# Three passes of 256 columns against one of 512 and one of 256, on a float32r transformer kernel

## The chip, the core and the metric

The kernel runs on one core of a Trainium2 chip. TensorE multiplies (a weight load of 128 columns, then a pass in which the moving columns stream through), VectorE and ScalarE do elementwise work, GpSimd a few small powers, SyncE issues the loads of the weights. The metric is the device time of one execution in microseconds. The profile is that of one execution, with the span from its first to its last instruction.

## The reference

Two layers of a hybrid block and then two layers of a second block run over 256 tokens of width 1024, all in float32. What matters here is the matrix products; cut to them:

```python
h = modulate(rms_norm(x, norm1_g), shift1, scale1)          # first block, two layers
(rq, rk, rv, rg, gq, gk, gv, glr, gg, fq, fk, fv, ff) = split(h @ w_in)
...                                                          # retention, gated linear attention, fox attention
y_br = einsum('bsnw,nwd->bsnd', branches, w_br)
mixed = sum(sigmoid(h @ w_mg + b_mg) * y_br, axis=2) @ w_o
u, g = split(h2 @ w_up); u = causal_dwconv(u, w_conv, b_conv)
x = x + gate2 * ((silu(u) * g) @ w_down)                     # width 2816 in between
...
x = layer_norm(ALPHA * x + 0.5 * swiglu(x, wg, wu, wd))      # second block: twice per layer, a mixer between them
x = x + sigmoid(x @ ple_wg + b) * (p @ ple_wp)               # "ple" part
```

The modulation vectors (shift, scale, gate) are a matrix-vector product of the condition with `w_ada`.

## The kernel before

TensorE's fast format is float32r. To keep float32's accuracy, each operand is split into a high part in float32r and a low part, the rounded rest: weights as `wh` (ScalarE, L284) and `wl` (VectorE, L285), activations as a pair of tiles, `hh`/`hl` for the normed input, `bh`/`bl` for the input of a unit behind a norm, `hidh`/`hidl` for the hidden layer, `brh`/`brl`, `mxh`/`mxl`, `yh`/`yl`, `ph`/`pl` elsewhere. `mm3` (L329 to L331) then makes three passes, high x high, high x low and low x high, which add up in one PSUM region:

```python
mm(ps, wh, xh, start=first, stop=False, skip_group_check=True)
mm(ps, wh, xl, start=False, stop=False, skip_group_check=True)
i = mm(ps, wl, xh, start=False, stop=last, skip_group_check=True)
```

The work is cut into units of 256 output columns. A unit runs over 8 k-tiles of 128 rows (22 in the down projections), with two halves of 128 features each, so that a k-tile of a unit is two weight tiles of 128x128 and six passes. Kind F keeps features on partitions (the weights are loaded, 256 tokens stream); kind T keeps tokens on partitions (the activations are loaded, 256 weight columns stream), for the fox queries, keys and values and for the other values. A unit's sum stands in a tile `psg` of one PSUM bank, of which there are four, and a function (evac) takes it from there: a sigmoid, a convolution, a product, an update of the residual `x`. The other four banks are `psm` tiles, for the small products of the mixers. `pair_body` runs two units k-tile by k-tile. The first units behind a norm (`first_pair`) use `psw` tiles of 258 columns and are corrected by the norm's statistics afterwards (`norm_stats`, L490).

Weights come by DMA into six `raw` buffers of 512 KB, are split in chunks of 512 columns into ten pairs of `wh`/`wl`, and a chunk is asked for four chunks ahead. Extra work stands between the units: in the first block's gate stretch, and in its feed-forward, modulation products (`ada`, VectorE, L397), one 512 KB load each, whose results are needed later. In a gate block three gate units are followed by three branch units of 4 k-tiles each (`ybr`). Generators (`spawn`, `tick`) put the attention cores' small products in between the k-tiles. The instructions of an engine run in the order in which the tile framework puts them, and wait there for semaphores.

The order in a layer of the first block is: gated units behind the norm, the fox queries (a pair T), a small unit of 24 passes (`w_sm`), fox keys and values, the gated linear attention's units, the retention's units, four gate blocks, `w_o`, the feed-forward (22 up units, 4 down units).

## Time and profile before

| | |
|---|---|
| runs | 2084.49, 2087.77, 2089.73 us (median 2087.77) |
| profiled execution, span | 2080.2 us (no other time of it is recorded) |
| mean granted TensorE clock | 0.992 |
| TensorE busy | 2029.3 us, 16832 passes |
| VectorE busy | 1528.7 us |
| ScalarE busy | 1203.1 us |
| DMA | 402.87 MB, mean 194 GB/s |

Busy shares are unions of an engine's instructions. Successive matmuls overlap in the records (each lasts 280 ns or so), so that the pace of passes is to be read from the distance of their starts.

### The profile page before, as it was taken

The page shows a single profiled execution, that of the slowest core. Times are in us where ns is not written, and L with a number is a line of the kernel's source. Part 1 is how long each engine was busy: PE and PEld are TensorE (multiplying, and loading weights), DVE is VectorE, ACT ScalarE, POOL GpSimd, SP SyncE. Part 2 cuts the span into 40 slices and gives each one's busy share as a digit, 9 for nine tenths or more (in the row PEclk, how much of TensorE's full clock was granted, in tenths as well). Part 3 has the DMA queues.
Part 4 walks back from the last instruction along what each step waited for, and adds up shares of the span by engine and source line. Part 5 has one row for each costly group of instructions (what it writes and reads, how often), then busy time and mean ns, then how long its engine had stood idle before and what let it go on. Part 6 is the DMA issues. An engine that isn't in the chain of part 4 may idle for free.

```text
span 2080.2 us, 42872 instructions
## 1 busy us (share of the span) xinstructions
PE 2029.3 (98%) x16832; PEld 1996.0 (96%) x16832; DVE 1528.7 (73%) x2966; ACT 1203.1 (58%) x2268; POOL 42.3 (2%) x46
## 2 busy tenths in 40 slices
PE   6999999999999999999999999999999999999998
PEld 5999999999999999999999999999999998899998
DVE  7768789987668789865656798656765687587657
ACT  4755456555655456654555676555655586366545
POOL 0000000000000000000000000000000000000000
PEclk8999999999999999999999999999999999999999
DMA  8646876885546876765556436665566544246553
GB/s 314 203 142 230 279 255 220 291 277 182 166 143 231 280 251 220 226 180 191 187 179 187 156 117 203 185 185 169 193 187 182 178 153 123 82 147 193 182 171 105
DMA packets 123344, 402.87 MB, mean 194 GB/s; under 512 B 16994, under 2 KB 24452, under 8 KB 122884
## 3 DMA queue, kind: packets, MB, share of 16 engines
q1 hardware_dynamic: 112724, 396.71, 59.4%
q10 hardware_dynamic: 10416, 3.41, 0.7%
q8 instruction: 132, 2.16, 0.4%
q14 instruction: 72, 0.59, 0.1%
HBM read 396.79 MB, written 3.28 MB: 192 GB/s over the span
## 4 chain that ended last, share of the span: by engine, by line
PE 88%; DVE 6%; DMA 4%; issue 1%; POOL 1%; ACT 1%; SPq 0%; DVEq 0%; ACTq 0%; POOLq 0%
PE psg L329 26%; PE psg L330 26%; PE psg L331 26%; DMA raw<-w_ada 2%; PE psw L329 1%; PE psw L330 1%; PE psw L331 1%; DVE wl L285 1%; PE psm L1637 1%; DVE raw L397 1%; PE psm L1732 1%; PE psm L941 1%; DMA xx<-dx 1%; PE psm L1072 0%; DMA dx<-xb 0%
## 5 line engine op out<-in xcount | busy, mean ns | idle before, releaser
L284 ACT CAST wh<-raw 128x512 fp32r<-128x512 f32 (+1 forms) x1296 | 777.5, 616 | 641.3 <-PE psg L330 443.9
L285 DVE TENSOR_TENSOR wl<-raw,wh 128x512 fp32r<-128x512 f32 (+1 forms) x1296 | 867.0, 685 | 352.4 <-ACT wh L284 336.9
L330 PE MATMUL psg<-hl,wh 128*128 128x256 f32 x2328 | 652.8, 281 | 1.5 <-DVE hl L383 1.4
L329 PE MATMUL psg<-hh,wh 128*128 128x256 f32 x2328 | 653.0, 281 | 0.8 <-DVE gate L1180 0.8
L331 PE MATMUL psg<-hh,wl 128*128 128x256 f32 x2328 | 651.4, 280 | 1.3 <-DVE wl L285 1.3
L329 PEld LDWEIGHTS psg<-hh,wh 128*128 128x128 f32 x2328 | 437.8, 188 | 3.3 <-issue 2.0
L330 PEld LDWEIGHTS psg<-hl,wh 128*128 128x128 f32 x2328 | 438.2, 188 | 2.3 <-DVE hl L383 1.6
L331 PEld LDWEIGHTS psg<-hh,wl 128*128 128x128 f32 x2328 | 437.0, 188 | 1.7 <-DVE wl L285 1.5
L329 PE MATMUL psg<-hidh,wh 128*128 128x256 f32 x1056 | 297.2, 281 | 0.0
L330 PE MATMUL psg<-hidl,wh 128*128 128x256 f32 x1056 | 297.1, 281 | 0.0
L331 PE MATMUL psg<-hidh,wl 128*128 128x256 f32 x1056 | 297.1, 281 | 0.0
L329 PEld LDWEIGHTS psg<-hidh,wh 128*128 128x128 f32 x1056 | 198.8, 188 | 0.0
L331 PEld LDWEIGHTS psg<-hidh,wl 128*128 128x128 f32 x1056 | 198.8, 188 | 0.0
L330 PEld LDWEIGHTS psg<-hidl,wh 128*128 128x128 f32 x1056 | 198.8, 188 | 0.0
L330 PE MATMUL psg<-bl,wh 128*128 128x256 f32 x704 | 197.8, 281 | 0.2 <-DVE bl L383 0.2
L331 PE MATMUL psg<-bh,wl 128*128 128x256 f32 x704 | 197.6, 281 | 0.0
L329 PE MATMUL psg<-bh,wh 128*128 128x256 f32 x704 | 197.6, 281 | 0.0
L397 DVE CUSTOM_DVE_ANT_0 raw<-raw,cact,par 128x1024 f32<-128x1024 f32 x96 | 122.8, 1280 | 50.1 <-DMA raw<-w_ada 50.0
L330 PEld LDWEIGHTS psg<-bl,wh 128*128 128x128 f32 x704 | 132.8, 189 | 0.5 <-DVE bl L383 0.4
L329 PEld LDWEIGHTS psg<-bh,wh 128*128 128x128 f32 x704 | 132.8, 189 | 0.0
L331 PEld LDWEIGHTS psg<-bh,wl 128*128 128x128 f32 x704 | 132.6, 188 | 0.0
L329 PE MATMUL psg<-wh,hh 128*128 128x256 f32 (+1 forms) x368 | 106.5, 290 | 0.0
(436 smaller groups left out, 3007.5 us busy)
## 6 DMA issues: line engine op xcount, KB each, us to landing
raw<-f_up SPq DMA_DIRECT2D x176, 512.0 KB, 4.5
raw<-w_ada SPq DMA_DIRECT2D x96, 512.0 KB, 5.1
raw<-w_up SPq DMA_DIRECT2D x88, 512.0 KB, 5.2
raw<-w_in SPq DMA_DIRECT2D x80, 512.0 KB, 4.5
raw<-f_dn SPq DMA_DIRECT2D x80, 512.0 KB, 3.6
raw<-w_mg SPq DMA_DIRECT2D x48, 512.0 KB, 4.7
raw<-w_down SPq DMA_DIRECT2D x40, 512.0 KB, 3.8
raw<-c_in SPq DMA_DIRECT2D x32, 512.0 KB, 4.2
```

The costliest lines, as they stand in the source:

```text
L284: self.A.copy(out=wh[:, :e], in_=r)
L285: self.V.tensor_tensor(out=wl[:, :e], in0=r, in1=wh[:, :e].bitcast(F32), op=SUB)
L329: mm(ps, wh, xh, start=first, stop=False, skip_group_check=True)
L330: mm(ps, wh, xl, start=False, stop=False, skip_group_check=True)
L331: i = mm(ps, wl, xh, start=False, stop=last, skip_group_check=True)
L397: i = self.V.tensor_tensor_reduce(out=w, in0=w, in1=self.cact, scale=1.0, scalar=self.P(f"b_ada{l}", j), op0=MULT, op1=ADD, accum_out=self ...
L941: mm = lambda o, l_, r_, s, e: PE.matmul(o, l_, r_, start=s, stop=e, skip_group_check=True)
L1637: mm = lambda o, l_, r_, s: PE.matmul(o, l_, r_, start=s, stop=True, skip_group_check=True)
L1732: PE.matmul(p[:, i, :], l_(i, h), r_(i, h), start=(i == 0), stop=True, skip_group_check=True)
```

## The change

The two parts of an activation stand in one tile, `x[:, 0]` high and `x[:, 1]` low (`hx`, `bx`, `hidx`, `brx`, `mxx`, `yx`, `px`). A new kind A streams both through a weight tile in one pass of 512 columns, so that the first half of a PSUM bank gets high x high and the second half high x low, and adds low x high into the second half. Behind the unit `summed` copies the second half out of PSUM on ScalarE and adds the first on VectorE (tile `sm`), and the evac reads that. A `psg` tile is now two banks, and there are two of them. Kind T units are 512 columns wide and keep three passes; so do branch units, the small unit and the units behind a norm (kinds F and `mm3`). The weight pairs are eight in place of ten. The fox queries, keys, and the values are each one unit of 512 columns, with `both` and `whole` as their evacs. `down` and `wo` update `x` from `sm`; `ln_add` updates `x` twice from PSUM.

```diff
-    WB = 10
+    WB = 8
...
-        self.pg = pool("psg", bufs=4, space=PSUM)
+        self.pg = pool("psg", bufs=2, space=PSUM)
...
+    def mm2(self, ps, wh, wl, x, first, last):
+        self.mm(ps, wh, x, start=first, stop=False)
+        return self.mm(ps[:, 1, :], wl, x[:, 0, :], start=False, stop=last)
...
+    def kA(self, acc, wh, wl, x, first, last):
+        for m, ps in enumerate(acc):
+            sl = slice(m * 128, (m + 1) * 128)
+            self.mm2(ps, wh[:, sl], wl[:, sl], x, first, last)
...
+    def halves(self, t):
+        return [t[:, m, :].rearrange("p (z t) -> p z t", z=2) for m in range(2)]
+
+    def summed(self, u, out=None, scale=1.0):
+        acc, t = u
+        if out is None:
+            out = self.np_.tile([128, 2, S], F32, name="sm", tag="sm", bufs=3)
+        for hi, lo, o in self.parts(u, out):
+            if scale == 1.0:
+                self.A.copy(out=o, in_=lo)
+                self.V.tensor_tensor(out=o, in0=o, in1=hi, op=ADD)
...
-        return self.pg.tile([128, 2, S], F32, name="psg", tag="g")
+        return self.pg.tile([128, 2, 512], F32, name="psg", tag="g")
...
-        pa, pb = self.psG(), self.psG()
+        t = self.psG()
+        ua = (self.halves(t), t)
+        ub = ([self.psM((128, 2, S)) for _ in range(2)], None)
...
+    def ln_add(self, mp):
+        def fn(u):
+            x2 = self.x[:, 2 * mp:2 * mp + 2, :]
+            for hi, lo, x in self.parts(u, x2):
+                self.V.scalar_tensor_tensor(x, x, ALPHA, hi, MULT, ADD)
+                self.V.tensor_tensor(out=x, in0=x, in1=lo, op=ADD)
+            self.norm_add(mp)
...
-        self.pair(wi(0), wi(1), fox_qk("qF", 0, 0), fox_qk("qF", 1, 0), "T")
-        self.one(self.w(f"w_sm{l}", 0, 8, 128), small, m_n=1)
-        self.one(wi(2), fox_qk("kF", 0, 6), "T")
-        self.one(wi(3), fox_qk("kF", 1, 6), "T")
+        self.one(wt(0), both(fox_qk, "qF", 0), "T")
+        self.one(self.w(f"w_sm{l}", 0, 8, 128), small, "F", m_n=1)
+        self.one(wt(1), both(fox_qk, "kF", 6), "T")
```

How this moves instructions is shown at three places. The first is TensorE where a gate unit of the first layer ends and the first branch unit (`brh`, `brl`, then `brx`) begins; before:

```order
L331 MATMUL psg<-hh,wl 128x256
L329 MATMUL psg<-hh,wh 128x256
L330 MATMUL psg<-hl,wh 128x256
L331 MATMUL psg<-hh,wl 128x256
L329 MATMUL psg<-brh,wh 128x256
L330 MATMUL psg<-brl,wh 128x256
L331 MATMUL psg<-brh,wl 128x256
```

and of the change (L333 is `mm`, through which all passes go):

```order
L333 MATMUL psg<-hx,wh 128x512
L333 MATMUL psg<-hx,wl 128x256
L333 MATMUL psg<-hx,wh 128x512
L333 MATMUL psg<-hx,wl 128x256
L333 MATMUL psg<-brx,wh 128x256 x2
L333 MATMUL psg<-brx,wl 128x256
```

Two passes of the gate unit have become one of 512 columns; the branch unit still has three per weight tile. The second place is VectorE in the first layer's feed-forward, for a pair of units with two modulation products (`ISA raw,mod`); before:

```order
L285 TENSOR_TENSOR wl<-raw,wh 128x512 x2
L383 TENSOR_TENSOR hidl<-hid,hidh 128x512
L718 SCALAR_TENSOR_TENSOR conv<-psg,par,conv 128x255
L285 TENSOR_TENSOR wl<-raw,wh 128x512
L719 SCALAR_TENSOR_TENSOR conv<-psg,par,conv 128x254
L718 SCALAR_TENSOR_TENSOR conv<-psg,par,conv 128x255
L285 TENSOR_TENSOR wl<-raw,wh 128x512
L719 SCALAR_TENSOR_TENSOR conv<-psg,par,conv 128x254
L397 ISA raw,mod_82<-raw,cact,par 128x1024
L397 ISA mod_82 128x1
L285 TENSOR_TENSOR wl<-raw,wh 128x512
L728 TENSOR_TENSOR hid<-act,psg 128x512
```

and of the change:

```order
L404 TENSOR_TENSOR sm<-sm,psg 128x512
L290 TENSOR_TENSOR wl<-raw,wh 128x512
L450 ISA raw,mod_82<-raw,cact,par 128x1024
L450 ISA mod_82 128x1
L785 SCALAR_TENSOR_TENSOR conv<-sm,par,conv 128x255 x2
L786 SCALAR_TENSOR_TENSOR conv<-sm,par,conv 128x254 x2
L290 TENSOR_TENSOR wl<-raw,wh 128x512 x3
L404 TENSOR_TENSOR sm<-sm,psg 128x512
L290 TENSOR_TENSOR wl<-raw,wh 128x512
L795 TENSOR_TENSOR hid<-act,sm 128x512
```

An add (`sm`) has come ahead of each unit's evac, and everything else of it is still there. The third place is TensorE in the first layer around the small unit behind the fox queries; before, the query pair, the small unit and the keys follow each other with nothing between, and the turned queries (`w_486`, `w_496`, the two halves) stand later, within the keys:

```order
L330 MATMUL psg<-wl,hh 128x256
L331 MATMUL psg<-wh,hl 128x256
L903 MATMUL psm<-ident,w_486 128x128 x4
L903 MATMUL psm<-ident,w_496 128x128 x4
L329 MATMUL psg<-wh,hh 128x256
```

and of the change, from the end of the query unit over the small unit to the start of the key unit:

```order
L333 MATMUL psg<-wl,hx 128x512
L333 MATMUL psg<-wh,hx 128x512
L333 MATMUL psg<-hx,wh 128x256 x2
L333 MATMUL psg<-hx,wl 128x256
...
L333 MATMUL psg<-hx,wl 128x256
L975 MATMUL psm<-ident,w_434 128x128 x4
L333 MATMUL psg<-wh,hx 128x512
L333 MATMUL psg<-wl,hx 128x512
```

The turned first half of the queries (`w_434`) now stands ahead of the first pass of the keys.

## Rows read from the trace of the kernel before

**Rows 1.** The page, part 1: busy time and share of each engine.
```profile
PE 2029.3 (98%) x16832; PEld 1996.0 (96%) x16832; DVE 1528.7 (73%) x2966; ACT 1203.1 (58%) x2268; POOL 42.3 (2%) x46
```

**Rows 2.** Table of stretches: length, busy PE, PEld, DVE, ACT, POOL, clock, DMA share, GB/s.
```profile
139.20:181.30 42.10, 40.40 (x334) 39.58 (x332) 36.25 (x63) 22.24 (x38) 1.01 (x1) 1.00 0.59 190
206.90:232.40 25.50, 25.50 (x219) 25.50 (x218) 21.12 (x37) 11.98 (x25) 0.00 (x0) 1.00 0.86 290
306.40:322.60 16.20, 14.19 (x107) 13.98 (x106) 13.82 (x29) 9.47 (x20) 1.67 (x1) 0.89 0.63 212
322.60:435.70 113.10, 113.10 (x963) 113.10 (x962) 104.50 (x198) 66.66 (x129) 0.00 (x0) 1.00 0.81 271
...
791.10:904.20 113.10, 113.10 (x963) 113.10 (x962) 95.36 (x175) 73.45 (x133) 0.00 (x0) 1.00 0.69 216
...
966.80:1092.30 125.50, 125.50 (x1059) 125.50 (x1058) 75.02 (x122) 66.20 (x110) 0.00 (x0) 1.00 0.59 184
...
1683.50:1853.20 169.70, 157.28 (x1310) 152.31 (x1309) 124.66 (x334) 98.66 (x216) 11.62 (x9) 0.97 0.40 122
```

**Rows 3.** Timeline of TensorE: start, us, operation; steady stream, first and 23rd pass.
```profile
1675.79 0.28 PE L329 MATMUL psg<-hh,wh 128*128 128x256 f32 x1
...
1678.38 0.28 PE L330 MATMUL psg<-hl,wh 128*128 128x256 f32 x1
```

**Rows 4.** Timeline of TensorE: weights of 16 columns, first and 21st pass.
```profile
1679.96 0.28 PE L329 MATMUL psm<-hh,wh 128*16 128x256 f32 x1
...
1682.23 0.28 PE L331 MATMUL psm<-hh,wl 128*16 128x256 f32 x1
```

**Rows 5.** Timeline of TensorE: first passes of 128 columns behind longer ones.
```profile
1170.05 0.22 PE L329 MATMUL psg<-wh,hh 128*128 128x128 f32 x1
1170.11 0.28 PE L330 MATMUL psg<-wl,hh 128*128 128x128 f32 x1
```

**Rows 6.** Timeline of TensorE: token-major unit, first and ninth pass.
```profile
525.00 0.28 PE L330 MATMUL psg<-wl,hh 128*128 128x256 f32 x1
...
525.91 0.28 PE L329 MATMUL psg<-wh,hh 128*128 128x256 f32 x1
```

**Rows 7.** Timeline of TensorE: full float32 matmuls of 256 columns, ten and four in a row.
```profile
1203.88 2.32 PE L1306 MATMUL psm<-xb,bd 128*128 128x256 f32 x10
...
1206.74 1.02 PE L1306 MATMUL psm<-xb,bd 128*128 128x256 f32 x4
```

**Rows 8.** VectorE: timeline in the first feed-forward; all its waits for modulation weights.
```profile
360.50 1.28 DVE L397 CUSTOM_DVE_ANT_0 raw<-raw,cact,par 128x1024 f32<-128x1024 f32 x1
...
362.81 2.49 DVE L285 TENSOR_TENSOR wl<-raw,wh 128x512 fp32r<-128x512 f32 x4
...
DVE raw L397 <- DMA raw<-w_ada: 50.0, 22, 4.6
```

**Rows 9.** Timelines of TensorE, ScalarE, VectorE: small unit, fox queries leaving PSUM.
```profile
522.05 0.28 PE L329 MATMUL psg<-hh,wh 128*128 128x256 f32 x1
...
524.88 0.28 PE L329 MATMUL psg<-wh,hh 128*128 128x256 f32 x1
...
521.54 0.60 ACT L848 ACTIVATE w<-psg 128x512 f32<-128x512 f32 x1 [1.50 <-PE psg L331]
...
524.10 0.60 ACT L848 ACTIVATE w<-psg 128x512 f32<-128x512 f32 x1
...
528.55 0.69 DVE L896 TENSOR_TENSOR w<-psg,hr 128x512 f32<-128x512 f32 x1 [0.74 <-POOL hr L389]
```

**Rows 10.** Waits of TensorE: for what, us in total, times, longest.
```profile
PE psm L490 <- DVE sq L478: 9.0, 3, 4.8
```

**Rows 11.** Groups of instructions: residual update, busy us, mean ns, idle before.
```profile
L802 DVE SCALAR_TENSOR_TENSOR x<-x,psg 128x256 f32<-128x256 f32 x48 | 18.1, 418 | 4.8 <-PE psg L331 4.8
```

**Rows 12.** Timelines of ScalarE and VectorE: the end of the program.
```profile
2073.60 1.60 ACT L828 ACTIVATE sig<-psg,par 128x256 f32<-128x256 f32 x4 [1.54 <-PE psg L331]
...
2076.53 0.69 DVE L830 TENSOR_TENSOR x<-sig,x 128x512 f32<-128x512 f32 x1
```

More of the change, by code (lines that the diff above doesn't have):

```diff
@@ L185 @@
 class Prog:
-    DCH = 4
-    CH = 2
+    DMAX = 1024
     RAW = 6
-    WB = 10
+    WB = 8
     AHEAD = 4
@@ L243, in w, with ch @@
         ap, out = self.io[name][u], []
-        for k in range(0, kt, self.DCH):
-            kk = min(self.DCH, kt - k)
+        ch = self.ch(n)
+        dch = 2 * ch
+        for k in range(0, kt, dch):
+            kk = min(dch, kt - k)
             load = {"ap": ap[:, k * n:(k + kk) * n], "n": kk * n}
-            out += [("w", load, h * n, min(self.CH, kk - h), n) for h in range(0, kk, self.CH)]
+            out += [("w", load, h * n, min(ch, kk - h), n) for h in range(0, kk, ch)]
         return out
+    def ch(self, n=256):
+        return min(2, self.DMAX // 2 // n)
     def dump(self, name, t):
@@ L362, in unit, with parts @@
                 self.kT(*a)
+        return ps
+    def halves(self, t):
[8 more added lines that the diff above has]
+                self.V.tensor_tensor(out=o, in0=o, in1=hi, op=ADD)
+            else:
+                self.A.activation(o, lo, AF.Copy, scale=scale)
+                self.V.scalar_tensor_tensor(o, hi, scale, o, MULT, ADD)
+        return out
+    def parts(self, u, out):
+        acc, t = u
+        if t is None:
+            return [(a[:, 0, :], a[:, 1, :], out[:, m, :]) for m, a in enumerate(acc)]
+        return [(t[:, :, 0:S], t[:, :, S:2 * S], out)]
     def queue(self, on=True):
@@ L578, in corrected, with first_sums @@
         return c
+    def first_sums(self):
+        t = self.psG()
+        self.nk["st"], self.nk["sp"] = self.psM(), self.psM()
+        return [[t[:, m, 0:S + 2] for m in range(2)], [self.psM()[:, 0:S + 2] for _ in range(2)]]
     def first_pair(self, ca, cb, fa, fb, mid=None, at=(2, 3)):
@@ L627, in fn @@
             xg, g, b = nk["bh"], nk["g"], nk["b"]
-            pm = [[pool.tile([128, S + 2], F32, name="psw", tag=tag) for _ in range(2)] for pool, tag in ((self.pg, "g"), (self.pm, "m"))]
+            pm = st["pm"]
             for k in range(8):
@@ L757, in ffn_first @@
         for mp in range(4):
-            self.one(self.w(f"w_down{l}", mp, KF), down(mp), xs=lambda: (st["hh"], st["hl"]))
+            self.one(self.w(f"w_down{l}", mp, KF), down(mp), xs=lambda: st["h"])
         self.close(es)
@@ L820, in keep, with fn @@
         def keep(mp):
-            return lambda ps: self.A.copy(out=st["pp"][:, 2 * mp:2 * mp + 2, :], in_=ps)
+            def fn(u):
+                self.summed(u, st["pp"][:, 2 * mp:2 * mp + 2, :])
+            fn.raw = True
+            return fn
         def gate(mp):
@@ L906, in fox_qk, with whole @@
             return fn
-        def keepT(dst, u, n=512):
+        def whole(dst):
             def fn(ps):
-                if u == 0:
-                    b[dst] = T([128, 2, n], F32, "vT" if n == 512 else dst, 2 if n == 512 else 1)
-                A.copy(out=b[dst][:, :, u * 256:(u + 1) * 256], in_=ps)
+                b[dst] = T([128, 2, 512], F32, "vT", 2)
+                A.copy(out=b[dst], in_=ps)
             return fn
@@ L1127, in mix @@
         self.step([], cores)
-        self.one(wi(6), gq)
-        self.one(wi(7), gk, "T")
-        self.one(wi(8), keepT("gv", 0), "T")
-        self.one(wi(9), keepT("gv", 1), "T")
+        self.one(wi(0), gq)
+        self.one(wi(1), gk, "T")
+        self.one(wt(3), whole("gv"), "T")
         def core(*gens):
@@ L1333, in fn @@
                     b["ge"] = T([128, 4, S], F32, "ge")
-                A.copy(out=b["ge"][:, 2 * u:2 * u + 2, :], in_=ps)
+                self.summed(ps, b["ge"][:, 2 * u:2 * u + 2, :])
+            fn.raw = True
             return fn
@@ L1453, in out_proj @@
         w = [self.w(name, mp) for mp in range(4)]
-        f = [lambda ps, mp=mp: self.ln_add(ps, mp) for mp in range(4)]
+        f = [self.ln_add(mp) for mp in range(4)]
         self.pair(w[0], w[1], f[0], f[1], xs=xs, settle=4)
```

237 lines of the change are left out of this document (124 added, 113 removed).

## The prediction, made blind

> **What bounds the kernel now.** The first view is the page's table of engines: TensorE is busy for 2029.3 of 2080.2 us [rows 1]. The table of stretches shows that this holds nearly everywhere: in the twenty units of a feed-forward part, from 322.6 to 435.7, 960 weight passes and three more take 113.1 us, 117.8 ns each, with no idle time at all [rows 2]. So the time is the number of passes times their pace, wherever VectorE, ScalarE and DMA keep up. VectorE is the next engine. The same table is to be read for it: 104.5 of 113.1 us in that stretch, 95.4 in its twin of the second layer (791.1), 21.1 of 25.5 in a block of gate and branch units (206.9), 36.3 of 42.1 in the retention stretch (139.2), but only 75.0 of 125.5 in the feed-forward of the second block (966.8) [rows 2]. What a faster TensorE is worth is therefore to be asked stretch by stretch.
>
> **How long a pass takes.** The product of one weight tile is three passes of 256 columns, each with its own weight load. In the steady stream 22 passes take 2.59 us, 118 ns each [rows 3]; 256 columns at the granted 2.4 GHz would be 106.7, so some 11 ns a pass are not columns. Loading 16 weight columns in place of 128 leaves 20 passes in 2.27 us, 113.5 each [rows 4]. A pass of 128 columns whose weights lie ready is followed after 60 ns by the next [rows 5]. Token-major passes run at 114 (eight in 0.91 us) [rows 6] to 118; I take 116.
>
> The new 512-column pass stands in no row. From below: full float32 matmuls of 256 columns, which stream twice as long as those above, follow each other at 216 ns (six more in 1.30 us) [rows 7]. From above: two passes at today's pace, 236. The line through 60 ns at 128 columns and 113.5 at 256 gives 220 at 512; a surcharge that grows with the columns gives 227. I take 222, since the two nearest rows are of the same number format. The 256-column pass behind it keeps between 113.5 and 118; I take 116. So a weight tile costs 338 ns in place of 3 x 118.3 = 355, with bounds of 330 and 354. The Trainium skill (TensorE: Matmul & The Clock Gate, Back-to-back issue gap) gives a pass its columns at 2.4 GHz and 2.5 ns: 109 and 216, where [rows 3] shows 118 for the first. By the page a tile would come down to 325 and the edit be worth 129 us; the row speaks against its small surcharge here.
>
> **The change part by part.** *Fewer passes.* 4288 weight tiles become a 512 and a 256 pass: 4288 x 17 ns = 72.9 us. 960 token-major passes become 480 of 512 columns: 960 x 116 - 480 x 222 = 4.8 us. Branch units, the small units and the units behind a norm keep three passes. Together 77.7 us, if nothing else were in the way. Per unit of sixteen tiles it is 0.27 us.
>
> *The second sum.* 182 units now end with a ScalarE copy of 512 columns out of PSUM (0.60 us, as the like-sized activation in [rows 9]) and a VectorE add (0.60, the step of four equal operations that take 2.49 [rows 8]); 14 more do it in halves and some twenty more into their own tiles; residual updates are an update and an add of 512 in place of two of 256 at 418 ns [rows 11], 0.5 us more. That is some 130 us on VectorE.
> - In the feed-forward of the second block and all down projections (2400 tiles, 40.8 us) it is hidden: VectorE would be at 75.0 + 22 x 0.6 = 88 of 119 us. The gain stays.
> - In the feed-forward stretch from 322.6 VectorE holds two 1.28 us modulation products per pair of units as well [rows 8]. 104.5 + 12.1 = 116.6 us of work, and some 2.5 us of waits that remain, give 119 where TensorE would need 107.7: the 5.4 us are not had and 6 are lost, -11.4.
> - Its twin has 107.5 against 107.7; of 5.4 I take off 1.4.
> - Eight gate blocks: 21.1 + 1.8 = 22.9 of 24.7, and VectorE waits there for modulation weights (50.0 us in 22 waits, up to 4.6 [rows 8]) with the adds queued behind. I give the 24 gate units nothing: -6.5.
> - Retention stretches: 36.3 + 7 x 0.6 = 40.5 of a TensorE time of 40: -4.6 for both layers.
> - The delta-rule mixer idles TensorE for 12 of 169.7 us [rows 2], waiting for chains that the change does not shorten: -3.9; the other mixer -2.
>
> *Two double PSUM tiles in place of four.* A unit must now wait until the unit before last has left its tile. With 5.4 us between, the 1.3 us of copy and add fit. They do not where a short unit stands between: the small unit behind the fox queries. Today its 24 passes last from 522.05 to 524.88; the two halves of the queries leave PSUM by a chain over ScalarE, VectorE and GpSimd from 521.54 to 529.24 [rows 9]. In the new order both halves hold one tile, and the second unit of the keys wants it back at the small unit's end: 0.25 + 7.7 - 2.8 = 5.1 us of idle TensorE per layer, bounds 2.5 and 6. Where TensorE idled 2.0 us of 16.2 the granted clock fell to 0.89, another 1.8 us [rows 2]. Twice 6.9: -13.8. The two-tile projections of the ple parts last 1.35 us and wait alike for sums behind the norm's work: -4 (bounds 0 and 8).
>
> *Longer chains.* Behind the mixers' output projections the statistics already hold TensorE up (9.0 us in three waits [rows 10]); copy and add put 1.3 us there, twice; six layer norms get 0.55 each: -5.9. At the end ScalarE takes 1.60 us for four sigmoids and VectorE finishes at 2077.2 [rows 12]; the copies ahead of them cost 1.5.
>
> *Sum.* 77.7 - 11.4 - 1.4 - 6.5 - 4.6 - 5.9 - 13.8 - 4 - 5.9 - 1.5 = 22.7 us. The profiled execution's span of 2080.2 becomes 2057.5. The runs' median, 2087.8, lies 7.6 above that span, which I put down to what lies around it and carry over: 2065.
>
> **The rivals.** *The passes run at their stream time.* If 512 columns take the 216 of [rows 7] and the other pass 113.5, a tile costs 329.5. The 8.5 ns more count where VectorE leaves room, some 2900 tiles: 25 us, and 3 in the token-major units. 2065 - 28 = 2037. For it speaks that loads hide behind a 512-long stream; against it, that the surcharge in [rows 4] stayed when nearly the whole load was gone.
>
> *The pace does not change with the length.* If the 11 ns grow with the columns, the long pass costs 236, a tile 354, and 4288 x 1 = 4 us are all that is gained, while the losses that are not merely missing gains stay (6 + 0.8 + 13.8 + 4 + 5.9 + 1.5 and some 2 in the mixers, 34). 2088 + 30 = 2118. [rows 5] speaks against it: from 128 to 256 columns the time does not quite double.
>
> *PSUM runs out.* This is the one that would make it slower with the passes as forecast. In the gate blocks three short branch units stand in a row, 2.84 us each, and their products sit in VectorE's queue behind modulation products that wait up to 4.6 us for their weights [rows 8]; with two tiles TensorE stands as soon as such a wait exceeds some 1.5 us. At 3 us per block and 1 us per pair in the first feed-forward it is 8 x 3 + 10 = 34 us: 2099. Four tiles absorb this today. The Trainium skill (Trainium Kernel Development and Optimization, Best Practices) says that consistent bubbles can mean that PSUM ran out; no row here shows such bubbles yet.
>
> **How the numbers follow.** The forecast case (2045 to 2081) gets 0.50, the fast passes 0.17, the case of PSUM 0.13, the unchanged pace 0.08; 0.12 is left for losses that just eat the gain. The time is the forecast's, 2065. The range from 2030 to 2100 leaves out the lower part of the fast case, the unchanged pace and the upper part of the PSUM case, about 0.18; the likeliest case's own range is 2045 to 2081. About 0.3%, 6.3 us, is what a measurement of this kernel can tell from no change. Faster 0.50 + 0.17 = 0.67, same 0.12, slower 0.13 + 0.08 = 0.21.
>
> **What would show it.** In the changed profile: a 512 pass to the next at 220 to 224 and the other at 114 to 118; feed-forward stretches of the second block at 119 us for 22 units; the stretch of the first feed-forward no shorter than 113, with TensorE waiting for split weights or for adds; an idle of 4 to 6 us ahead of the fox keys in each layer. Wrong would make me: a 512 pass outside 216 to 228; adds that VectorE delays by more than a unit, to be seen as TensorE waiting for them all over; or modulation products that slide out of the first feed-forward, so that VectorE does not bind there.

## The result, and the profile after

The changed kernel takes 2117.91 us (median of 4 runs, 2117.59 to 2118.36) where the kernel before, on the same chip, takes 2086.13 (2080.15 to 2089.73): a ratio of 1.0164, 95% interval 1.0139 to 1.0189. It is slower by 1.6%; the prediction was 2065 us, faster, with a range up to 2100. The profiled execution has a span of 2116.0 us and a mean granted clock of 0.986 (before: 2080.2 and 0.992).

The page's first part answers to [rows 1]:

```profile
PE 2027.1 (96%) x12064; PEld 1770.6 (84%) x12064; DVE 1666.1 (79%) x3148; ACT 1319.5 (62%) x2474; POOL 46.2 (2%) x46
```

TensorE has 4768 passes less and is busy for 2.2 us less. Its idle time, span less busy, went from 50.9 to 88.9 us. VectorE has 137.4 us more, where the prediction gave the second sum some 130, and ScalarE 116.4. The table of stretches of the changed kernel, with the columns of [rows 2]: a branch unit's stretch (three units of four tiles), the pair behind the first mixing part, the first feed-forward part, its twin, the first feed-forward part of the second block, then the pair behind a layer norm and the delta-rule mixer.

```profile
227.40:237.70 10.30, 8.97 (x74) 8.55 (x72) 8.98 (x17) 6.61 (x14) 0.00 (x0) 1.00 0.99 364
...
312.80:325.90 13.10, 12.89 (x107) 12.58 (x106) 12.42 (x28) 8.75 (x18) 1.07 (x1) 1.00 0.70 232
325.90:452.80 126.90, 116.36 (x642) 98.01 (x640) 119.17 (x221) 80.43 (x152) 0.00 (x0) 0.99 0.74 243
...
808.50:926.70 118.20, 113.97 (x643) 98.45 (x642) 108.07 (x199) 83.78 (x152) 0.00 (x0) 1.00 0.66 212
...
988.50:1112.20 123.70, 123.70 (x707) 108.03 (x706) 87.02 (x135) 77.39 (x134) 0.00 (x0) 1.00 0.57 186
...
1678.28:1696.33 18.05, 13.75 (x114) 13.37 (x113) 13.69 (x32) 10.18 (x19) 3.25 (x4) 1.00 0.45 138
1696.33:1884.62 188.29, 174.90 (x1161) 155.27 (x1162) 150.15 (x386) 125.12 (x267) 12.27 (x9) 0.95 0.36 115
```

Of the kernel before, the same branch stretch and the same pair behind the layer norm:

```profile
223.85:232.39 8.54, 8.54 (x74) 8.54 (x73) 6.11 (x10) 2.60 (x5) 0.00 (x0) 1.00 0.80 259
...
1653.34:1666.78 13.44, 13.44 (x114) 13.36 (x113) 11.30 (x25) 8.42 (x16) 2.88 (x4) 1.00 0.61 186
```

Two things are to be read here. Where nothing disturbs, the gain is small: the second block's first feed-forward part, in which TensorE is busy for the whole 123.70 us (the undisturbed stretch in what follows), has 352 tiles in that time where [rows 2] has 125.50, 5.1 ns a tile, against the 17 that the prediction took. And the largest losses stand in stretches where VectorE is nearly full: 113.1 became 126.9 with VectorE busy for 119.2, its twin 118.2 with 108.1. The pair behind the layer norm took 13.44 us before and takes 18.05; the branch stretch took 8.54 and takes 10.30 (six of eight such stretches grew, by 0.4 to 1.8 us). The pair behind the mixing part gained 3.1 us on [rows 2].

Stage by stage the two profiles differ so: the first block's feed-forward parts took 13.8 and 5.1 us more, the branch units 7.8 in all, three pairs behind layer norms 10.8, the ple parts 3.3, and three other stages 5.6 together. The two pairs behind the mixing parts took 6.5 us less, the second block's first two feed-forward parts 2.7.

The timeline of TensorE in the undisturbed stretch, one tile (start, us, operation), answers to [rows 3]:

```profile
1030.21 0.40 PE L333 MATMUL psg<-bx,wh 128*128 128x512 f32 x1
1030.45 0.28 PE L333 MATMUL psg<-bx,wl 128*128 128x256 f32 x1
1030.57 0.39 PE L333 MATMUL psg<-bx,wh 128*128 128x512 f32 x1
```

Behind the long pass the next one starts after 0.24 us, behind the short one after 0.12; over the whole stretch the means are 233 and 118 ns. TensorE's waits in the changed kernel (for what, us in total, times, longest) answer to [rows 10]:

```profile
PE psg L333 <- DVE wl L290: 13.8, 15, 1.6
PE psg L333 <- DVE sm L404: 10.1, 6, 5.8
PE psg L333 <- DVE hx L423: 9.4, 5, 3.4
PE psg L702 <- ACT xg L698: 6.4, 5, 2.8
PE psm L543 <- DVE sq L531: 5.4, 1, 5.4
```

Four of the five are waits for VectorE: for split weights (`wl`), the second sum (`sm`), the normed residual (`hx`), the sums of squares. The one for ScalarE (`xg`) was there before too, with 6.1 us. In the first feed-forward part TensorE idles for some 10.5 us: 6.9 of it for split weights, and 3.7 for the first weights of the down projection:

```profile
PE psg L333 <- DVE wl L290: 6.9, 9, 1.5
...
452.82 0.79 PE L333 MATMUL psg<-hidx,wh 128*128 128x512 f32 x1 [3.70 <-ACT wh L289]
```

The load of these was issued late, at 445.88, since SyncE waited for products and conversions to free a buffer, so that this wait too goes back to VectorE. The groups of instructions (busy, mean ns, idle before) price the second sum's two steps at 681 and 580 ns:

```profile
L404 DVE TENSOR_TENSOR sm<-sm,psg 128x512 f32<-128x512 f32 x182 | 123.9, 681 | 3.3 <-ACT sm L403 3.1
L403 ACT COPY sm<-psg 128x512 f32<-128x512 f32 x182 | 105.5, 580 | 16.9 <-PE psg L333 16.9
```

### The profile page after: what moved, and what is told of

The parts are those of the page before. It is cut to its first block, busy times and chain, and to the rows that moved or that the text cites. A ratio compares the mean times of both kernels' runs of the same rounds, so it can differ in the third digit from the quotient of the medians.

```text
span 2116.0 us, 33633 instructions
## 1 busy us (share of the span) xinstructions
PE 2027.1 (96%) x12064; PEld 1770.6 (84%) x12064; DVE 1666.1 (79%) x3148; ACT 1319.5 (62%) x2474; POOL 46.2 (2%) x46
## 4 chain that ended last, share of the span: by engine, by line
PE 78%; DVE 10%; DMA 6%; ACT 4%; issue 1%; POOL 1%; SPq 0%; ACTq 0%; DVEq 0%; POOLq 0%
PE psg L333 65%; PE psm L333 5%; DVE wl L290 3%; DMA raw<-w_up 3%; DVE raw L450 2%; ACT wh L289 1%; PE psm L1710 1%; DVE sm L404 1%; PE psm L1811 1%; PE psm L1012 1%; POOL hr L442 1%; DMA raw<-w_br 1%; DMA raw<-w_ada 1%; DMA raw<-w_mg 1%; PE psm L1144 1%
## 5 line engine op out<-in xcount | busy, mean ns | idle before, releaser
L333 PE MATMUL psg<-hx,wh 128*128 128x512 f32 (+1 forms) x2208 | 784.4, 396 | 17.8 <-DVE hx L423 9.4
L333 PE MATMUL psg<-hx,wl 128*128 128x256 f32 x2184 | 624.9, 286 | 12.3 <-DVE wl L290 12.2
L333 PEld LDWEIGHTS psg<-hx,wh 128*128 128x128 f32 x2208 | 416.4, 189 | 112.1 <-issue 11.4
L333 PEld LDWEIGHTS psg<-hx,wl 128*128 128x128 f32 x2184 | 414.2, 190 | 20.5 <-DVE wl L290 19.5
L333 PE MATMUL psg<-hidx,wh 128*128 128x512 f32 x1056 | 373.2, 396 | 3.7 <-ACT wh L289 3.7
L333 PE MATMUL psg<-hidx,wl 128*128 128x256 f32 x1056 | 299.9, 284 | 0.0
L333 PE MATMUL psg<-bx,wh 128*128 128x512 f32 (+1 forms) x928 | 283.1, 362 | 2.5 <-DVE bx L436 2.5
L333 PEld LDWEIGHTS psg<-hidx,wh 128*128 128x128 f32 x1056 | 199.5, 189 | 49.9 <-ACT wh L289 4.0
L333 PE MATMUL psg<-bx,wl 128*128 128x256 f32 (+1 forms) x784 | 220.6, 281 | 0.0
L333 PEld LDWEIGHTS psg<-hidx,wl 128*128 128x128 f32 x1056 | 200.0, 189 | 0.4 <-DVE wl L290 0.4
L333 PEld LDWEIGHTS psg<-bx,wh 128*128 128x128 f32 x928 | 165.1, 189 | 32.3 <-DVE bx L436 2.0
L333 PEld LDWEIGHTS psg<-bx,wl 128*128 128x128 f32 x784 | 148.0, 189 | 0.0
L333 PE MATMUL psg<-wh,hx 128*128 128x512 f32 (+2 forms) x416 | 129.2, 379 | 1.1 <-ACT qF L976 0.9
L333 PEld LDWEIGHTS psg<-wh,hx 128*128 128x128 f32 x416 | 77.1, 190 | 17.7 <-issue 3.0
L333 PE MATMUL psm<-bx,wh 128*128 128x258 f32 (+1 forms) x352 | 79.0, 304 | 0.0
L333 PE MATMUL psg<-wl,hx 128*128 128x512 f32 (+2 forms) x208 | 77.2, 371 | 0.0
L333 PE MATMUL psg<-brx,wh 128*128 128x256 f32 x384 | 69.9, 284 | 4.3 <-DVE sm L404 4.3
```

What stands on the lines that cost most here:

```text
L333: i = self.PE.matmul(*a, start=start, stop=stop, skip_group_check=True)
```

## The experiments

Open were: A, the pace of the long pass itself, or B, other engines that hold it up; S, the second sum's work on VectorE and ScalarE; P (called C at first), two accumulator tiles of two banks in place of four of one; W, eight weight buffers in place of ten. Ratios are to the kernel before, run beside each. Differences below are between medians, each taken from the kernel before in its own group of runs.

**e1, passes by themselves.** Streams of 40 passes, one form after another.

```diff
+        for i in range(n):
+            PE.matmul(pz, w(i), xr[:, :, i % 8, :], start=(i == 0), stop=False)
+            PE.matmul(pz[:, 1, :], w(i + 1), xr[:, 0, i % 8, :], start=False, stop=(i == n - 1))
```

> Streams of 40 TensorE passes of one shape each, nothing beside them except in the last three; the layers are left out, so the output is not the model's. Theory A (a float32r pass costs by its columns, with no fixed part to save): 128, 256, 384 and 512 columns step at about 59, 118, 176 and 233 ns, so two 256-column passes cost what one of 512 does, and 512 columns over 16 weight columns also take about 233. Rival B (the long pass would run at about 222 and the kernel's other engines hold it up): 512 columns alone step at 216 to 223 ns, and one of the three last streams, with VectorE, ScalarE or DMA beside it, goes back to about 233.

The timeline of its TensorE (start of a stream, us, form, number of passes):

```profile
31.32 4.58 PE L53 MATMUL pn<-xr,wr 128*128 128x128 f32 x40
35.74 5.01 PE L57 MATMUL pn<-xr,wr 128*128 128x256 f32 x40
40.59 7.14 PE L61 MATMUL pn<-xr,wr 128*128 128x384 f32 x40
47.57 9.27 PE L65 MATMUL pn<-xr,wr 128*128 128x512 f32 x40
56.68 9.23 PE L70 MATMUL pstr<-xr,wr 128*128 128x512 f32 x40
65.74 9.41 PE L74 MATMUL pw<-xr,wr 128*16 128x512 f32 x40
74.99 4.72 PE L78 MATMUL pw16n<-xr,wr 128*16 128x256 f32 x40
...
97.83 0.39 PE L91 MATMUL pmix<-xr,wr 128*128 128x512 f32 x1
...
111.60 0.40 PE L91 MATMUL pmix<-xr,wr 128*128 128x512 f32 x1
...
111.95 8.81 PE L96 MATMUL pbf<-xb,wb 128*128 128x512 bf16 x40
120.60 4.53 PE L101 MATMUL pbf<-xb,wb 128*128 128x256 bf16 x40
124.88 9.34 PE L110 MATMUL pdve<-xr,wr 128*128 128x512 f32 x40
134.06 9.23 PE L117 MATMUL pact<-xr,wr 128*128 128x512 f32 x40
143.13 9.23 PE L124 MATMUL pdma<-xr,wr 128*128 128x512 f32 x40
```

The distance of two streams' starts over 40 is the step: 110.5 ns at 128 columns, 121.3 at 256 (119.9 without a first step of 170), 174.5 at 384, 227.8 at 512. So three passes of 256 alone cost 364, and 227.8 + 121.3 would be 349. But the 39 tiles from 97.83 to 111.60, long and short pass in turn, take 353.1 each: 236.5 for the long pass and 116.6 for the short one. Neither theory holds whole: the long pass by itself does save a little, yet it does not come to the 222 of the prediction, and alternating costs 4 ns more than the two apart. B falls: with VectorE, ScalarE or DMA beside it the step is 229.5 (227 but for one start after 314), 226.8 and about the same again. The pace is the pass's own.

**e2, e3, e6: joined or three passes, with and without the second sum.** All keep the two large accumulator tiles and the eight weight buffers. (In the edits, `...` stands for lines or arguments left out.)

```diff
# e2
-            if scale == 1.0:
-                self.A.copy(out=o, in_=lo)
-                self.V.tensor_tensor(out=o, in0=o, in1=hi, op=ADD)
...
+            self.A.activation(o, hi, AF.Copy, scale=scale)
...
-        f(u) if getattr(f, "raw", False) else f(self.summed(u))
...
+            f(u[1][:, :, 0:S])
# e3
-        self.mm(ps, wh, x, start=first, stop=False)
+        self.mm(ps[:, 0, :], wh, x[:, 0, :], start=first, stop=False)
+        self.mm(ps[:, 1, :], wh, x[:, 1, :], start=False, stop=False)
# e6
-            self.mm2(ps, wh[:, sl], wl[:, sl], x, first, last)
+            self.mm3(acc[:, m, :], wh[:, sl], wl[:, sl], x[:, 0, :], x[:, 1, :], ...)
```

> The changed kernel without the second sum: what the low half holds is left out of every feature-major unit, and the evacuation reads the high half as before. TensorE's passes, the PSUM tiles and the token-major units stay as changed. Theory A (the long pass saves next to nothing, the second sum's work costs all of the loss): 2070 to 2088 us, first FFN with the modulation products beside it back to about 113 us. Rival C (two large PSUM tiles in place of four cost it): 2105 us or more, since they stay.

> The changed kernel with three 256-column passes again where it has one of 512 and one of 256; the two sums and everything behind them stay. Theory A: a tile costs 354 to 356 ns either way, so 2116 to 2130 us, within 0.6% of the changed kernel. If the joined pass had saved the 17 ns a tile that the prediction took (4288 tiles, 72.9 us) and something else had eaten it, this run would be about 2180 to 2190 us.

> Three 256-column passes into one sum as before the change, nothing added behind them; the changed PSUM tiles (two of two banks), the smaller weight pool and the 512-column token-major units stay. Theory A: the loss goes with the second sum, 2075 to 2090 us. Rival C (PSUM tiles): 2105 us or more.

| against the kernel before | no second sum | second sum |
|---|---|---|
| three passes | e6: 2142.12 us, 1.0276 (1.0251 to 1.0301) | e3: 2150.63 us, 1.0318 (1.0294 to 1.0341) |
| joined pass | e2: 2113.02 us, 1.0141 (1.0113 to 1.0169) | changed kernel: 1.0164 (1.0139 to 1.0189) |

This turned my first reading over. e2 and e6 came out as the rival P had it; e3, at 2150.63, lies between what its two theories gave (2116 to 2130 and 2180 to 2190). Without a second sum most of the loss stays (e2, e6), so S alone is not it; e6, three passes into one sum, is the kernel before with other accumulators, eight weight buffers and wider token-major units, and it loses 58.6 us. In this table the second sum costs 8.5 us with three passes and 2.3 with joined ones; the joined pass gains 29.1 and 35.3. Of this gain 22 us are the 5.1 ns of 4288 tiles; the rest was not assigned to a cause. The price of the second sum is a net one: without it the evac reads PSUM itself (last lines of e2's edit) and holds the accumulator until it is through. In e2 the first feed-forward part takes 118.29 us, and waits for the convolution:

```profile
330.36:448.65 118.29, 114.93 (x642) 99.53 (x641) 111.06 (x211) 75.04 (x141) 0.00 (x0) 0.99 0.79 273
...
PE psg L333 <- DVE conv L786: 3.0, 2, 2.2
```

So 5.2 of the 13.8 us by which this part grew come without any second sum there. The table of stretches of e6, the first feed-forward part and the undisturbed one, and its TensorE's longest wait in the first:

```profile
341.33:465.84 124.51, 116.79 (x962) 115.84 (x961) 112.42 (x218) 76.29 (x140) 0.00 (x0) 0.99 0.79 264
...
1014.10:1139.55 125.45, 125.45 (x1058) 125.45 (x1057) 74.52 (x112) 66.69 (x110) 0.00 (x0) 1.00 0.58 184
```
```profile
PE psg L333 <- DVE conv L771: 7.7, 5, 2.1
```

The first part loses 11.4 us here, most of it to the same wait: for an accumulator that the convolution on VectorE still reads.

**e4, e7: the two buffer counts by themselves**, in the kernel before.

```diff
# e4
-        self.pg = pool("psg", bufs=4, space=PSUM)
+        self.pg = pool("psg", bufs=2, space=PSUM)
...
-        pa, pb = self.psG(), self.psG()
+        pa, pb = self.psG(), self.psM((128, 2, S))
# e7
-    WB = 10
+    WB = 8
```

> The kernel before with two psg tiles in place of four (the second unit of a pair takes a psm tile), nothing else changed. Theory P (two units' worth of accumulators leave no slack, so a late evacuation stops TensorE): 2105 to 2145 us, with the loss in the first feed-forward parts, the branch units and the token-major units. Theory S (the second sum costs the loss) and theory W (eight weight buffers in place of ten cost it): 2078 to 2092 us, as before.

> The kernel before with eight pairs of split weight buffers in place of ten, nothing else changed. Theory W: 2105 us or more. Theories P and S: 2075 to 2092 us; the first pair behind the mixing part may lose some of its 2.0 us of idle, since fewer weight conversions can stand ahead of the last residual update on VectorE.

e4 took 2129.94 us, 1.0235 (1.0204 to 1.0266); e7 2096.27 us, 1.0064 (1.0041 to 1.0086). 46.9 and 13.2 us make 60.1, and e6, which has both, lost 58.6: in total P and W account for e6. Stretch by stretch they don't simply add. The first feed-forward part took 113.1 us before, 117.83 in e4, 115.95 in e7 and 124.51 in e6. The pairs behind the mixing parts were faster in both (13.4 and 13.6 us in e4, 12.41 twice in e7, where 16.2 stood before):

```profile
334.05:451.88 117.83, 114.65 (x962) 113.43 (x961) 111.92 (x222) 74.73 (x140) 0.00 (x0) 1.00 0.80 275
...
311.02:323.43 12.41, 12.41 (x107) 12.41 (x106) 11.18 (x26) 7.97 (x16) 1.09 (x1) 1.00 0.66 211
323.43:439.38 115.95, 113.90 (x962) 113.28 (x961) 105.97 (x202) 68.89 (x132) 0.00 (x0) 1.00 0.78 267
```

e7's time went outside what both theories said of it, between them. One branch stretch of e4 shows what a stop costs beyond itself:

```profile
229.73:245.17 15.44, 11.13 (x74) 10.93 (x73) 11.68 (x22) 4.55 (x10) 0.00 (x0) 0.81 0.87 287
```

TensorE idles for 4.3 us there, the granted clock is 0.81, and 74 passes that took 8.5 us take 11.1.

**e5, e5b: 80 of the 96 modulation products left out**, of the changed kernel and of the one before.

```diff
-            i = self.V.tensor_tensor_reduce(out=w, in0=w, in1=self.cact, ...)
+            if l == 0 and j < 16:
...
+            else:
+                i = self.V.tensor_copy(out=self.mod[l][:, j:j + 1], in_=w[:, 0:1])
```

> The changed kernel with the modulation's multiply-and-reduce left out for all but the first 16 columns (a copy of one column stands in its place; its loads stay), so 80 times 1.28 us of VectorE work less beside the first block. If VectorE's queue is what the first feed-forward part waits for: 126.9 us back to 113 to 115, and 2090 to 2105 us in all. If loads or the transfers' pace set it: the part stays above 122 us, and 2110 us or more.

> The kernel before with the same 80 multiply-and-reduce instructions left out (a one-column copy in their place, loads kept). If the products cost the changed kernel time only because its second sum has filled VectorE beside them: 2070 to 2084 us here, a gain of at most 13 us (the idle of the first pairs behind the mixing parts), against 28.9 us in the changed kernel. If they cost by themselves: about 2055 us.

e5 took 2088.99 us, 1.0025 (1.0014 to 1.0036); e5b 2075.07 us, 0.9956 (0.9941 to 0.9970). e5 came out 1 us below the range of its first theory, e5b within it. The products cost the changed kernel 25.9 us (31.8 - 5.9) and the one before 8.5. Of the 25.9, the first feed-forward part gets 14.4, its twin 5.4, the branch units 6.6. In e5 the first feed-forward part is at the undisturbed pace, 320 tiles and what goes with them in 112.50 us, with its second sums in place:

```profile
320.42:432.92 112.50, 112.50 (x643) 98.44 (x641) 100.14 (x221) 84.14 (x158) 0.00 (x0) 1.00 0.83 294
```

So in the first block's feed-forward parts neither two accumulators nor the second sum stop TensorE by themselves; with the products beside them VectorE does. That is not the whole account: without products the change still costs 14.4 us (5.9 + 8.5), although its joined passes are worth 22, so that some 36 us of loss have nothing to do with products. They stand in the pairs behind the layer norms, the ple parts and the mixers among others.

**e10, accumulators given back in the feed-forward parts** of the changed kernel.

```diff
-        t = self.psG()
+        t = None if alt else self.psG()
...
-            acc = self.halves(t)
+            acc = [self.psM((128, 2, S)) for _ in range(2)] if alt else self.halves(t)
```

> The changed kernel with every other single unit of the four feed-forward parts accumulating in two psm tiles (idle there) instead of a psg tile: three to four units' worth of accumulators in these parts, sums in four instructions instead of two for such a unit. Theory P: the first feed-forward part goes from 126.9 us to 118 or less, its twin from 118.2 to 114 or less, 2095 to 2107 us in all. Theory S: both stay or grow, 2113 to 2125 us.

2122.42 us, 1.0189 (1.0164 to 1.0213): no gain, and the first part took 130.3 us. The sums of such a unit are four shorter instructions in place of two, and VectorE is busy for 120.5 us there in place of 119.2; that this is the cause was not shown:

```profile
323.72:454.00 130.28, 115.89 (x643) 97.51 (x641) 120.48 (x232) 81.51 (x161) 0.00 (x0) 1.00 0.71 236
```

So more accumulators do not help the changed kernel in these parts. Elsewhere (branch and token-major units) more accumulators were not tried in it.

**e13, e14, e15, e16: repairs of the changed kernel.** Ten weight buffers; products on GpSimd with their row sums on ScalarE; no second sum in the last unit ahead of a norm; all three.

```diff
# e13
-    WB = 8
+    WB = 10
...
-            out = self.np_.tile([128, 2, S], F32, name="sm", tag="sm", bufs=3)
+            out = self.np_.tile([128, 2, S], F32, name="sm", tag="n2", bufs=4)
# e14
+                self.G.tensor_tensor(out=w, in0=w, in1=self.cact, op=MULT)
+                i = self.A.activation(w, w, AF.Identity, bias=..., accum_out=self.mod[l][:, j:j + 1])
# e15
+            ..., self.ln_add(mp), kind="AAAF"[mp], ...
```

> The changed kernel with ten pairs of weight buffers again (the second sum's tiles take turns in the buffers of the norms' scratch, which makes the room). If the two buffers given up cost the changed kernel what they cost the kernel before by itself (13 us): 2100 to 2109 us. If VectorE's load hides it: 2113 to 2120 us.

> The changed kernel with 80 of its 96 modulation products off VectorE: GpSimd multiplies, ScalarE sums along the row; all else as changed. If VectorE's load is what the first block waits for: most of the 28.9 us that leaving the products out gave, 2088 to 2098 us, first feed-forward part at 115 us or less. If ScalarE, which gets a pass of 1024 columns for each, or GpSimd's pace holds it instead: 2105 us or more.

> The changed kernel with the last down unit of each feed-forward part in three passes into one sum, so that no second sum stands between it and the norm behind it. If the second sum's chain makes the first pairs behind the layer norms late: those that went +3.7, +4.6 and +2.5 us lose 2 us or more each where a feed-forward part stands before, 2106 to 2113 us. If the two accumulator tiles make them late: no change, 2116 to 2120 us.

> The edits of the three kernels before it together. If the costs found are separate and add up: about 45 us less than the changed kernel, 2066 to 2080 us, so faster than before the change. If the token-major and mixing parts still lose to the two accumulator tiles: 2085 us or more.

e13: 2125.98 us, 1.0202 (1.0180 to 1.0225). The first feed-forward part stayed at 126.0 us, so W does not rule there; the delta-rule mixer went from 188.3 to 199.7, likely because its scratch stands in the buffers that now also hold the sums, which no run separates. The time lies outside both ranges given for e13, so that what ten buffers are worth in the changed kernel is open. e14: 2202.83 us, 1.0574 (1.0554 to 1.0593). Its waits of TensorE and of ScalarE stand in the first fence, GpSimd's group of instructions in the second:

```profile
PE psg L336 <- DVE sm L407: 66.2, 27, 6.8
...
ACT raw L458 <- POOL raw L457: 89.7, 43, 4.9
```
```profile
L457 POOL TENSOR_TENSOR raw<-raw,cact 128x1024 f32<-128x1024 f32 x80 | 208.6, 2619 | 382.2 <-DMA raw<-w_ada 282.8 <-DVE wl L293 32.6 <-ACT sm L406 25.9
```

A product takes 2.62 us there, ScalarE waits for it 43 times, and its copies out of the accumulators stand behind that wait: TensorE waits 66.2 us for sums. The conversions on VectorE also lengthened, from 685 to 721 ns on the mean, and this mean hides two groups: the 67 that overlap a product on GpSimd last 1409 ns, the other 1229 last 683. The convolution's updates that have both inputs in SBUF go from 0.48 to 1.67 us beside a product; the second sum's add, with one input in PSUM, does not lengthen. A short and a long one of the same operation, and the product beside the long one:

```profile
366.05 0.87 DVE L793 SCALAR_TENSOR_TENSOR conv<-cor,par,conv 128x254 f32<-128x254 f32 x2
...
374.06 3.00 DVE L793 SCALAR_TENSOR_TENSOR conv<-sm,par,conv 128x254 f32<-128x254 f32 x2
374.13 2.65 POOL L457 TENSOR_TENSOR raw<-raw,cact 128x1024 f32<-128x1024 f32 x1 [1.34 <-DVE conv L792]
```

The Trainium skill (Perfetto Trace Analysis, Optimizing Scalar/DVE Operations) warns that moving work between VectorE and GpSimd might not help, as they share a port; this trace agrees, with 1409 ns beside a product and 683 without. Summed over all operations that overlap a product, VectorE has some 76 us more, an estimate from these durations. How the loss divides between the queue on ScalarE and the longer operations on VectorE was not shown.

e15: 2116.91 us, 1.0152 (1.0133 to 1.0171). Its pair behind a layer norm, and the mixer behind it:

```profile
1674.85:1688.49 13.64, 13.61 (x115) 13.31 (x113) 11.50 (x26) 8.62 (x17) 2.87 (x4) 1.00 0.58 176
1688.49:1884.00 195.51, 177.47 (x1160) 157.58 (x1161) 150.50 (x391) 126.81 (x270) 12.06 (x9) 0.94 0.35 111
```

18.05 became 13.64, so the second sum ahead of the norm was the cause of that late norm. But the mixer took 195.5 us where it took 188.3 (186.4 before): the gain was given back there, for a reason that no run shows, and in all nothing came of it, as e15's second theory had the total. The second sum is not all that this mixer loses to: e4 and e7, without one, have it at 193.2 and 194.1. e16 (2190.19 us, 1.0508, 1.0488 to 1.0528; in its second range) carries e14's loss, and does not tell whether the other two add.

**e9, e11, e12, e18, e19: the joined pass where it should pay.** e9 only reorders the kernel before. e11, e12, e18 and e19 put the joined pass into it where VectorE has room, with four accumulators and ten buffers.

```diff
# e9
+                    with self.tc.high_priority():
                         V.scalar_tensor_tensor(self.x[:, k, :], ps[:, j, :], ...)
# e11
-                self.one(ca, evac_g(j))
-                self.one(cb, evac_u(j))
+                self.joined(ca, evac_g(j), lambda: self.hx)
+                self.joined(cb, evac_u(j), lambda: self.hx)
...
+        for mp in range(3):
+            self.joined(self.w(f"f{f}_dn{l}", mp, KF), ...)
# e18
+                self.hx = nk["bx"][:, :, :, 0:S]
# e19
+        for mp in range(3):
+            self.joined(self.w(f"w_down{l}", mp, KF), down(mp), lambda: st["x"])
```

> The kernel before, with the last residual updates of the mixing parts put ahead of the weight conversions in VectorE's order. If those conversions are what the statistics wait for: the two first pairs behind go from 16.2 to about 13 us, 2074 to 2080 us in all. If the conversions put back are then waited for themselves: 2081 to 2086 us.

> The kernel before, ten weight buffers and four accumulator tiles kept, with the joined pass and the second sum in the second block's feed-forward parts alone, there only in single units and not in the last one ahead of a norm: 1680 tiles. At the 4.8 ns a tile that undisturbed stretches of the changed kernel show: 8 us less, 2073 to 2079 us. If a unit of two accumulator tiles leaves too little slack there, or the sums come too late: 2083 us or more.

> The edits of the two kernels before it together. If both gains are there and add: 2066 to 2074 us, 0.5 to 0.8% faster than before. If one of them is not: 2074 to 2082 us.

> As e11, with the first feed-forward part of the second block reading the residual's own high and low parts from one tile, as the single units there must. 2076 to 2081 us, 0.1 to 0.4% faster than before, if e11's gain of 4.4 us stands; 2083 us or more if the one tile for both parts adds waits.

> As e18, with three of the four down units of the first block's two feed-forward parts joined as well: 264 tiles more, 1.3 us less at 4.8 ns a tile, 2075 to 2080 us. If the second sum makes VectorE late where the first block still has products to do: no better than e18 or worse.

In e11 and e12 the single units of the second block's first feed-forward part read the tile of an earlier norm, of the same size, in place of the residual; e18 and e19 read the right one. e9: 2083.28 us, 0.9995 (0.9983 to 1.0007), in the range of its second theory: the first pair went from 16.2 to 14.3 us, the second stayed. e11: 2079.04, 0.9974 (0.9961 to 0.9987), at the edge of its first range. e12: 2078.22, 0.9973 (0.9963 to 0.9984), in its second range. e18: 2081.20, 0.9987 (0.9974 to 1.0000), just above its first range. e19: 2081.83, 0.9985 (0.9971 to 0.9999), no better than e18, as its second theory had it. The up units of the second block's first feed-forward part in e18:

```profile
967.56:1091.71 124.15, 124.15 (x771) 111.25 (x769) 87.18 (x156) 75.69 (x145) 0.00 (x0) 1.00 0.59 186
```

288 joined tiles bring 1.35 us on the 125.50 of [rows 2], 4.7 ns each, and none of the sums stops TensorE there. At that price the 1680 tiles of e18 would bring 7.9 us, and 2.4 were measured. The gain is there in this stretch, but in all it is 0.13%, below the 0.3% that this measurement can tell from no change. None of the versions that do all the work on the right data gains as much as 0.3% on the kernel before. Part of the difference stands in the first block's feed-forward parts, which keep three passes and yet took 113.9 us in place of 113.1; the rest is open.

## Why the prediction was wrong

**The step that failed: "I take 222 ... So a weight tile costs 338 ns in place of 3 x 118.3 = 355".** A tile costs 351 in undisturbed stretches, 233 for the long pass where 222 was taken and 118 for the short one where 116 was, and 353 in e1. The term mis-sized is the first of the sum: its 72.9 us were 22, and this is 51 of the 53 us by which the forecast missed. The prediction's own sign of being wrong, a long pass outside 216 to 228, is what came. That the other terms nearly cancel is luck: the losses were put at 55 us (77.7 - 22.7) and come to some 54 (31.8 + 22), but they stand in other places than forecast, as the parts below show. The ground of the 222 was the 60 ns of [rows 5], from which I drew a line; a stream of 128-column passes with weights of their own steps at 110.5 (e1), and the four passes right behind that row, which the view had too, step at 112:

```profile
1170.56 0.28 PE L331 MATMUL psg<-wh,hl 128*128 128x128 f32 x1
```

So the 60 ns were those of one pair of passes, and no pace to draw a line from. [rows 7] were of another number format. The 4.8 us of the token-major units went with it: their 480 passes, priced at 222, stepped at about 232 (median distance of starts in the trace).

**First feed-forward part, "-11.4".** The mechanism was right: VectorE, second sums and products together, ends last (e5, e10). VectorE was busy for 119.2 us, where I had 116.6 of work and 119 in all; but its work does not close up, and 126.9 stand there. Mis-sized by 7.9 us; the twin, given 107.7 + 1.4 = 109.1, takes 118.2, by 9.1. By e2 some 5 us of the first part's growth come without second sums, when the evacs hold the two accumulators instead.

**Second block, "hidden".** Right for its first feed-forward part: in the changed kernel TensorE is busy for 123.70 of 123.70 us there, and e18 shows it again with other accumulators. Behind the two mixers it was not so. The norm there came late, and the passes behind a wait of 2.76 us ran at a granted clock of 0.75:

```profile
1283.09:1290.00 6.91, 6.91 (x31) 5.96 (x32) 6.40 (x14) 5.68 (x15) 0.00 (x0) 0.75 0.20 68
```

The feed-forward parts behind the mixers took 114.0 us where 113.1 stood before.

**Two accumulator tiles.** The forecast priced them by one stall ahead of the fox keys, 2 x 6.9 us, and 4 in the ple parts. Ahead of the keys TensorE idles for 2.3 us in one layer and 1.7 in the other, where 5.1 stood; the ple parts took 3.3 us more, about as forecast. The rival had them run out for 34 us. In the kernel before they would cost 46.9 us by themselves (e4), so its cover by four tiles was rightly seen; in the changed kernel copy and add last 0.58 + 0.68 us, so that a tile can be free 1.3 us behind its unit where nothing queues ahead, and in the feed-forward parts e10 shows nothing of the cost. The gate units gained nothing, as forecast, and the branch units behind them grew by 7.8 us in all. e5, with the same two accumulators, brings seven of the eight stretches back to within 0.4 us of 8.5: products in VectorE's queue do it, as the rival had put it, at a third of its 24 us.

**Eight weight buffers** had no term. By themselves they cost 13.2 us in the kernel before (e7); e13 found none of it in the changed kernel's first feed-forward part, where 0.9 us came back (126.9 to 126.0).

**"... six layer norms get 0.55 each".** Three of them lost 3.7, 4.6 and 2.5 us. e15 shows for the second that the last unit's sum is the cause; the others stand behind mixers and kept theirs in e15, but in e2 and e6, without second sums, they are within 1.1 us of the kernel before. **"... copy and add put 1.3 us there, twice"** (behind the mixers' output projections) had the wrong sign: the pairs gained 3.1 and 3.3 us. In the kernel before, eight weight buffers alone (e7) take both to 12.41 us, and two accumulators alone (e4) to 13.4 and 13.6, so that each by itself is enough; in the changed kernel ten buffers (e13) give back 1.0 us of the gain in each. Which of VectorE's instructions the fewer buffers move was not shown. e9, which puts the residual updates ahead, has the first pair at 14.3 us and the second as before; e11 and e18, without that edit, have 14.4 in the first too, so that its effect is not shown either.

**The unchanged pace.** The rival that gave 2118, with a chance of 0.08, gave the time, and its tile of 354 was within 3 ns of the 351 measured. Its losses were not right: of 13.8 us ahead of the fox keys few came, the first feed-forward parts and the norms took more. That the total agrees is in part chance.

**The sum as it came out.** From [rows 1] to the page after, TensorE's busy time fell by 2.2 us in place of 22. The granted clock fell from 0.992 to 0.986 on the mean; TensorE was busy at the lower of its two levels (1.2 GHz) for 30.6 us before and for 41.8 after, and half of the 11.2 us, 5.6, is what this can have cost. The rest was not assigned. Idle time grew by 38.0. Of the 31.8 us of loss, the products' share beyond what they cost before, 25.9 - 8.5 = 17.4, is the largest part that a pair of runs shows; how the other 14.4 us divide among the norms, the accumulators and the weight buffers stays open.

## What to carry to other kernels

Before passes are joined to save a fixed cost, measure the joined pass in the sequence in which it will stand: here nearly all of a pass's time grew with its columns, and 4288 joined tiles were worth 22 us of 2086. (The 480 passes that the token-major units lost brought nothing: one of 512 columns takes as long as two of 256.) Price extra work on a second engine by what stands in its queue already: in one stretch the sums were free, and in the other, beside the products, the change cost more than it saved. And undo a change one resource at a time in both kernels: two accumulators in place of four cost the kernel before 47 us, and in the feed-forward parts of the changed one giving two back brought nothing.

## What the runs showed of the hardware that was not expected

Alone, float32r passes cost more than bf16 ones by a nearly constant amount: 227.8 ns against 216.3 at 512 columns ((120.60 - 111.95) / 40), 121.3 against 109 at 256 (4.53 us less the last pass's 0.27, over 39). Weights of 16 columns do not help the long pass (231.3), though they do help the short one (113.8, 4.55 us from 74.99 to the next stream over 40). A 512 and a 256 pass in turn cost 353.1, where the streams apart would give 349.1. A stop of 4.3 us in a stretch of 15.4 went with a granted clock of 0.81 (e4): behind it the passes stepped at 213 ns for some 6 us, which is the lower clock level, so that a wait cost more than half its length again. Operations of VectorE with both inputs in SBUF lasted twice as long and more while GpSimd multiplied (683 to 1409 ns, 0.48 to 1.67 us); 15 adds with one input in PSUM did not (e14).
